# Rotary and norm products of an input projection: GpSimd or VectorE

## The chip, the cores and the metric

The kernel runs on one core of one Trainium2 chip (trn2). The metric is the device time of one execution in microseconds; lower is better. Before the change three runs took 3346.41, 3346.62 and 3347.53 us, a median of 3346.62 us.

A core has five engines that run side by side, each with its own queue of instructions, in order: TensorE (PE in the profile; its weight loads are PEld), VectorE (DVE), ScalarE (ACT), GpSimd (POOL) and SyncE (SP, which here only starts DMAs). GpSimd starts some DMAs too.

## The reference

Two layers of a hybrid diffusion backbone work on 128 context tokens and 1024 latent tokens with 1024 features. Cut to what matters:

```python
def _rms_norm(x, w):
    y = x * lax.rsqrt(jnp.mean(x * x, axis=-1, keepdims=True) + NORM_EPS)
    return y * w

def _rope_1d(x, pos):                      # rotate-half rotary over d dims
    ...
    return jnp.concatenate([x1 * cos - x2 * sin, x1 * sin + x2 * cos], axis=-1)

def _layer(x, cond, p, pos, ctx_kv):
    ...
    h = _rms_norm(x, p['norm1']) * (1 + sc1) + sh1
    proj = h @ p['w_in']                   # 1024 -> 2048
    q, k, v, zc, zh = jnp.split(proj, IN_SPLITS, axis=-1)
    q = _rms_norm(q.reshape(b, L, N_HEADS, HEAD_DIM), p['q_norm'])
    k = _rms_norm(k.reshape(b, L, N_KV_HEADS, HEAD_DIM), p['k_norm'])
    ...
    if pos is not None:                    # latent tokens
        q = _rope_2d(q, rows, cols)
        k = _rope_2d(k, rows, cols)
    attn_out = _blocked_attention(q, keys, vals)
    conv_out = _conformer_conv(zc, p)
    hy_out = _hyena(zh, p)
    mix = jnp.concatenate([attn_out, conv_out, hy_out], axis=-1) @ p['w_o']
    x = x + g1 * mix
    h2 = _rms_norm(x, p['norm2']) * (1 + sc2) + sh2
    ...                                    # ConvFFN, w_up and w_down
```

## The kernel before, in words

All activations lie transposed: 1024 features as 8 chunks of 128 partitions, 1152 tokens (128 context, then 1024 latent) along the free dimension, in three segments of 384 columns (`SEG`). Segment 0 holds both kinds of tokens, which have different modulation, so work that depends on it is cut there into 128 and 256 columns (`PARTS`). A matmul in full precision is made of three: each operand is split into a high part (`hh`, `whi`), rounded by a cast, and a low part (`hl`, `wlo`), the rest; `mm3` (L243) adds high x high, high x low and low x high.

Each layer has four phases. `phase1` (L1162) is the **input projection**: the norm of x, then 16 output tiles of 128 features, in the order that `ORDER` gives: six for the Hyena, then a q (0), k (4), v (5), and so on. `phase2` is the attention with the convolution beside it, `phase3` the output projection, `phase4` the ConvFFN. In the profiled execution phase 1 runs from about 85 to 408 us in layer 0 and from 1751 to 2068 us in layer 1.

**The norm.** `norm_seg` (L434) goes through the 8 chunks of a segment. R holds 1/rms of every token in all partitions. For most chunks VectorE forms x * A * R (`nt`, L450), ScalarE adds the shift B with a cast to the high part (`hh`, L451), and VectorE forms the low part (`hl`, L452). For chunks 2 and 5 (`norm_pool`, L149) the route is another: GpSimd multiplies x by R (L444), ScalarE applies A and B (L446) and casts the high part (L235), and GpSimd subtracts for the low part (L238). `norm_seg` is called from `phase1` with `which` = 0 and from `phase4` with `which` = 1, through `normed_dense2`, whose matmuls on the first two output tiles follow the chunks as they come.

**The rotations.** q (four tiles of two heads) and k (one) are scaled by `normed` (L1068): ScalarE squares and copies the matmul's result, TensorE sums the squares over 64 features and spreads the reciprocal roots, VectorE multiplies (L1090). Then `rope_out` (L1053) rotates the latent tokens of a segment: VectorE shuffles partitions into `sh` (L1060), GpSimd forms x * cos (L1061) and `sh` * sin (L1062), VectorE adds (L1063), `hilo` casts on ScalarE and subtracts on VectorE, and two DMAs on SP's queue store the parts (L1065, L1066). It is called 15 times per layer, 5 times on 256 columns and 10 times on 384.

**Order.** The framework orders each engine's instructions when the kernel is built, by priorities and a simulated timeline of its own; `high_priority` moves some ahead. Engines then work their queues in order. `tick` (L1181) interleaves the projection's matmuls with the rotation's steps and with those of the Hyena, whose own transforms (`hy_conv`, L826) also run on TensorE, with adds and products on VectorE.

**The seam.** After output tile 9 `open_attention` (L1244) takes memory that the Hyena frees and loads K with DMAs on GpSimd's queue (L1253 to L1258); `maxes` (L1329) loads q on SP's queue and starts the score matmuls (`S`, L1356).

Of the kernel before, what the change touches and what calls it, by code (L numbers as in the profile page):

```python
# [17 lines left out]
L = 1024  # L18
# [118 lines left out]
class Kern:  # L137
# [296 lines left out]
    def norm_seg(self, l, which, x, rr, hh, hl, s):  # L434

        nc, sh, g = self.nc, 0 if which == 0 else 24, self.nc.gpsimd
        a, b = SEG[s]
        R = self.rms_rows(rr)
        for c in range(8):
            y, xc = self.N("nt", "nw", 4), x(c, a, b)  # L440
            hi, lo = hh[c][:, a:b], hl[c][:, a:b]
            AB = [(u - a, v - a, self.aff[l][:, which, cond, c : c + 1], self.modT[l][:, cond, sh + c : sh + c + 1]) for cond, u, v in PARTS[s]]
            if c in self.norm_pool:
                self.mul(y[:], xc, R[:], g)  # L444
                for u, v, A, B in AB:
                    self.act(y[:, u:v], y[:, u:v], AF.Identity, scale=A, bias=B)  # L446
                self.hilo(hi, lo, y[:], lo_eng=g)
            else:
                for u, v, A, B in AB:
                    self.stt(y[:, u:v], xc[:, u:v], A, R[:, u:v], ALU.mult, ALU.mult)  # L450
                    self.act(hi[:, u:v], y[:, u:v], AF.Identity, bias=B)  # L451
                    self.stt(lo[:, u:v], y[:, u:v], B, hi[:, u:v].bitcast(F32), ALU.add, ALU.subtract)  # L452
# [599 lines left out]

    def rope_out(self, l, x, s, dst):  # L1053

        nc, g = self.nc, self.nc.gpsimd
        o, (a, b) = (128, (0, 256)) if s == 0 else (0, ((256, 640), (640, 1024))[s - 1])
        n = b - a
        x = x[:, o : o + n]
        sh, hi, lo = (self.N(t, "rp", 4, dt) for t, dt in (("sh", F32), ("rh", F32R), ("rl", F32R)))
        nc.vector.stream_shuffle(sh[:, :n], x, [(k + 16) % 32 for k in range(32)])  # L1060
        self.mul(x, x, self.cs[:, a:b], g)  # L1061
        self.mul(sh[:, :n], sh[:, :n], self.cs[:, L + a : L + b], g)  # L1062
        self.add(x, x, sh[:, :n])  # L1063
        self.hilo(hi[:, :n], lo[:, :n], x)
        nc.sync.dma_start(dst(0, a, b), hi[:, :n].bitcast(F32))  # L1065
        nc.sync.dma_start(dst(1, a, b), lo[:, :n].bitcast(F32))  # L1066
# [817 lines left out]
```

## Time and profile before

| | |
|---|---|
| median of three runs | 3346.62 us (3346.41 to 3347.53) |
| the profiled execution | 3345.59 us |
| its span, first to last instruction | 3343.3 us |
| TensorE busy | 3134.0 us, 94% of the span |
| VectorE busy | 2160.7 us, 65% |
| ScalarE busy | 1195.1 us, 36% |
| GpSimd busy | 495.1 us, 15% |
| mean granted TensorE clock | 0.958 of full speed |

How to read it: the busy time of an engine is the sum over its instructions, waits and DMA starts left out. "Releaser" or "<-" names what ended a wait by the semaphores. PEclk is the TensorE clock that was granted, as a share of full speed; its two levels are 1.2 and 2.4 GHz. A group's mean is over instructions of one form and one tile name.

### The profile page before, as it was taken

The numbers are of one execution on the slowest core, as the hardware profiler recorded it, in microseconds if no ns is written. First come the engines' busy times: TensorE is split into PE (matmuls) and PEld (weight loads), VectorE is DVE, ScalarE is ACT, GpSimd is POOL, SyncE is SP. The second block draws the span as 40 slices with busy tenths as digits, with TensorE's granted clock in tenths as the row PEclk, the third lists the DMA queues.
The fourth block names the chain that finished last, engine by engine and source line by source line (L and its number), as shares of the span: only waits on it lengthen the run. The fifth ranks groups of instructions, "written<-read, shape, count | busy, mean of one in ns | idle before, by whom it ended". The sixth has DMA issues, their size and how long they took to land. (4 is left out here: it accounts for less than half of the span.)

```text
span 3343.3 us, 44669 instructions
## 1 busy us (share of the span) xinstructions
PE 3134.0 (94%) x17330; PEld 2769.0 (83%) x17330; DVE 2160.7 (65%) x3464; ACT 1195.1 (36%) x1976; POOL 495.1 (15%) x412
## 2 busy tenths in 40 slices
PE   5899778999799999999998997899999999999997
PEld 3899733449799999999998995345799999999997
DVE  6887889665765554545567896987365454554556
ACT  3433333452352222333344333435343233333223
POOL 5402234221310000000012113422110000000002
PEclk8899879999899999999999997899999999999998
DMA  7565544445311111111113446351511111111112
GB/s 280 172 224 173 158 151 168 156 161 163 127 38 42 42 44 43 42 42 44 42 56 134 161 142 212 100 164 61 190 29 51 42 42 43 43 42 42 42 44 70
DMA packets 152327, 336.08 MB, mean 101 GB/s; under 512 B 21360, under 2 KB 57844, under 8 KB 145589
## 3 DMA queue, kind: packets, MB, share of 16 engines
q1 hardware_dynamic: 147412, 318.69, 29.8%
q0 software_dynamic: 4704, 14.55, 1.5%
q8 instruction: 137, 2.24, 0.3%
q14 instruction: 74, 0.60, 0.1%
HBM read 264.86 MB, written 68.31 MB: 100 GB/s over the span
## 5 line engine op out<-in xcount | busy, mean ns | idle before, releaser
L241 PE MATMUL up<-hl,whi 128*128 128x384 f32 (+1 forms) x2112 | 712.8, 338 | 4.4 <-DVE hl L227 2.9
L241 PE MATMUL up<-hh,whi 128*128 128x384 f32 (+1 forms) x2112 | 710.3, 338 | 3.6 <-ACT hh L212 2.7
L241 PE MATMUL up<-hh,wlo 128*128 128x384 f32 (+1 forms) x2112 | 711.9, 337 | 0.0
L215 DVE TENSOR_TENSOR wlo<-wraw,whi 128x512 fp32r<-128x512 f32 x362 | 255.6, 706 | 646.6 <-ACT whi L235 646.3
L235 ACT CAST whi<-wraw 128x512 fp32r<-128x512 f32 x362 | 223.7, 618 | 848.2 <-PE dn L241 358.1
L241 PEld LDWEIGHTS up<-hl,whi 128*128 128x128 f32 x2112 | 398.7, 189 | 6.4 <-DVE hl L227 4.3
L241 PEld LDWEIGHTS up<-hh,whi 128*128 128x128 f32 x2112 | 398.7, 189 | 4.3 <-ACT hh L212 3.1
L241 PEld LDWEIGHTS up<-hh,wlo 128*128 128x128 f32 x2112 | 398.8, 189 | 0.0
L227 DVE SCALAR_TENSOR_TENSOR xt<-dn,mod,xt 128x128 f32<-128x128 f32 (+2 forms) x704 | 332.5, 514 | 71.3 <-PE dn L241 71.1
L241 PE MATMUL dn<-gh,wlo 128*128 128x384 f32 (+1 forms) x1056 | 359.0, 340 | 0.0
L241 PE MATMUL dn<-gh,whi 128*128 128x384 f32 (+1 forms) x1056 | 358.1, 339 | 0.0
L241 PE MATMUL dn<-gl,whi 128*128 128x384 f32 (+1 forms) x1056 | 357.4, 338 | 0.0
L227 DVE SCALAR_TENSOR_TENSOR fu<-pd,vec,fu 128x1154 f32<-128x1154 f32 (+2 forms) x192 | 254.0, 1324 | 91.7 <-ACT fu L212 89.2
L215 POOL TENSOR_TENSOR acc<-acc,sq 128x384 f32<-128x384 f32 x51 | 55.0, 1087 | 1633.2 <-ACT sq L212 1632.2
L241 PE MATMUL win<-hl,whi 128*128 128x384 f32 x768 | 265.0, 345 | 9.5 <-DVE hl L227 5.5
L241 PE MATMUL win<-hh,whi 128*128 128x384 f32 x768 | 264.0, 347 | 3.4 <-ACT hh L235 1.1
L241 PE MATMUL win<-hh,wlo 128*128 128x384 f32 x768 | 263.8, 344 | 0.0
L1357 DVE TENSOR_REDUCE mx<-S 128x1 f32<-128x384 f32 x384 | 196.6, 548 | 37.4 <-PE S L241 36.5
L1678 ACT COPY pd<-up 128x384 f32<-128x384 f32 (+1 forms) x352 | 131.8, 401 | 239.1 <-PE up L241 239.1
L212 ACT ACTIVATE p<-st 128x1024 f32<-128x1024 f32 x144 | 147.1, 1022 | 158.3 <-PE st L241 157.9
L241 PEld LDWEIGHTS dn<-gl,whi 128*128 128x128 f32 x1056 | 199.9, 189 | 0.0
L241 PEld LDWEIGHTS dn<-gh,whi 128*128 128x128 f32 x1056 | 199.7, 189 | 0.0
(294 smaller groups left out, 5196.7 us busy)
## 6 DMA issues: line engine op xcount, KB each, us to landing
wmod<-in_w_mod SPq DMA_DIRECT2D x48, 1024.0 KB
wraw<-in_w_up SPq DMA_DIRECT2D x176, 256.0 KB
wraw<-in_w_dn SPq DMA_DIRECT2D x88, 256.0 KB
wraw<-in_w_in SPq DMA_DIRECT2D x64, 256.0 KB
q<-qD SPq DMA_DIRECT2D x48, 256.0 KB
mh<-mixD SPq DMA_DIRECT2D x16, 576.0 KB
ml<-mixD SPq DMA_DIRECT2D x16, 576.0 KB
khD<-fK SPq DMA_DIRECT2D x16, 512.0 KB
```

Of the source, the lines that this page charges most:

```text
L212: return self.nc.scalar.activation(out, in_, f, **k)
L215: return (eng or self.nc.vector).tensor_tensor(out, a, b, op=op)
L227: return (eng or self.nc.vector).scalar_tensor_tensor(out, a, s, b, op0=op0, op1=op1)
L235: self.nc.scalar.copy(hi, src)
L241: self.nc.tensor.matmul(out, l, r, start=start, stop=stop)
L1357: nc.vector.tensor_reduce(m3[:, k, s : s + 1], S[:, :384], op=ALU.max, axis=AX.X)
L1678: self.nc.scalar.copy(p[:, u + o : v + o], t[:, u - a : v - a])
```

## The change

In `norm_seg` the route over GpSimd is taken only for `which` = 1, so in the input projection all 8 chunks go over VectorE and ScalarE. In `rope_out` both products go to VectorE. Nothing else changes; in phase 4 and at the end GpSimd keeps its share.

```diff
@@ -440,7 +440,7 @@
             y, xc = self.N("nt", "nw", 4), x(c, a, b)
             hi, lo = hh[c][:, a:b], hl[c][:, a:b]
             AB = [(u - a, v - a, self.aff[l][:, which, cond, c : c + 1], self.modT[l][:, cond, sh + c : sh + c + 1]) for cond, u, v in PARTS[s]]
-            if c in self.norm_pool:
+            if which and c in self.norm_pool:
                 self.mul(y[:], xc, R[:], g)
                 for u, v, A, B in AB:
                     self.act(y[:, u:v], y[:, u:v], AF.Identity, scale=A, bias=B)
@@ -1052,14 +1052,14 @@
     def rope_out(self, l, x, s, dst):
 
-        nc, g = self.nc, self.nc.gpsimd
+        nc = self.nc
         o, (a, b) = (128, (0, 256)) if s == 0 else (0, ((256, 640), (640, 1024))[s - 1])
         n = b - a
         x = x[:, o : o + n]
         sh, hi, lo = (self.N(t, "rp", 4, dt) for t, dt in (("sh", F32), ("rh", F32R), ("rl", F32R)))
         nc.vector.stream_shuffle(sh[:, :n], x, [(k + 16) % 32 for k in range(32)])
-        self.mul(x, x, self.cs[:, a:b], g)
-        self.mul(sh[:, :n], sh[:, :n], self.cs[:, L + a : L + b], g)
+        self.mul(x, x, self.cs[:, a:b])
+        self.mul(sh[:, :n], sh[:, :n], self.cs[:, L + a : L + b])
         self.add(x, x, sh[:, :n])
```

## Rows read from the trace of the kernel before

**Rows 1.** Page, busy time of each engine over the span
```profile
PE 3134.0 (94%) x17330; PEld 2769.0 (83%) x17330; DVE 2160.7 (65%) x3464; ACT 1195.1 (36%) x1976; POOL 495.1 (15%) x412
```

**Rows 2.** Windows view: stretch, its length, busy time (instructions) of PE, PEld, DVE, ACT, POOL; PEclk, DMA, GB/s
```profile
91.00:127.00 36.00, 32.65 (x150) 29.43 (x151) 32.45 (x66) 22.98 (x49) 17.25 (x14) 0.85 0.63 192
236.00:408.00 172.00, 158.18 (x1049) 149.22 (x1045) 143.82 (x268) 60.56 (x112) 38.23 (x36) 0.92 0.51 162
261.00:268.00 7.00, 6.03 (x24) 4.97 (x25) 4.55 (x11) 1.79 (x4) 3.36 (x3) 0.50 0.29 95
1751.00:1790.00 39.00, 29.36 (x142) 26.06 (x141) 37.23 (x62) 25.05 (x55) 19.82 (x20) 0.89 0.59 216
1850.00:2020.00 170.00, 169.69 (x1117) 165.01 (x1115) 140.97 (x242) 59.83 (x105) 19.02 (x21) 1.00 0.46 146
2043.00:2050.00 7.00, 3.54 (x12) 2.66 (x9) 2.87 (x6) 0.00 (x0) 0.71 (x2) 0.50 1.02 236
```

**Rows 3.** Waits of PE, 236 to 408 us: total, times, longest
```profile
PE iy L241 <- ACT zh L235: 2.2, 1, 2.2
```

**Rows 4.** Waits of PE, 1700 to 2090 us
```profile
PE win L241 <- DVE hl L227: 4.8, 5, 1.4
...
PE S L241 <- issue: 3.4, 1, 3.4
...
PE win L241 <- POOL raw L730: 1.6, 1, 1.6
...
PE win L241 <- POOL hl L215: 1.2, 2, 0.7
PE win L241 <- ACT hh L235: 1.1, 1, 1.1
```

**Rows 5.** Groups by form, DVE, 1750 to 1790 us: busy, mean ns, idle before
```profile
L227 DVE SCALAR_TENSOR_TENSOR nt<-xt,aff,rms 128x384 f32<-128x384 f32 x12 | 9.6, 826 | 0.2 <-ACT rms L431 0.2
L227 DVE SCALAR_TENSOR_TENSOR hl<-nt,mod,hh 128x384 fp32r<-128x384 f32 x12 | 8.6, 735 | 1.4 <-ACT hh L212 1.3
L227 DVE SCALAR_TENSOR_TENSOR hl<-nt,mod,hh 128x256 fp32r<-128x256 f32 x6 | 4.4, 725 | 0.0
L227 DVE SCALAR_TENSOR_TENSOR nt<-xt,aff,rms 128x128 f32<-128x128 f32 x6 | 3.8, 636 | 0.0
```

**Rows 6.** Groups by form, DVE, 91 to 127 us
```profile
L227 DVE SCALAR_TENSOR_TENSOR nt<-x,aff,rms 128x256 f32<-128x256 f32 x6 | 2.8, 472 | 0.0
...
L227 DVE SCALAR_TENSOR_TENSOR nt<-x,aff,rms 128x128 f32<-128x128 f32 x6 | 1.9, 336 | 1.0 <-DMA x<-in_xT 1.0
```

**Rows 7.** Timeline of DVE, 1786 to 1788 us: start, duration
```profile
1786.14 0.61 DVE L227 SCALAR_TENSOR_TENSOR hl<-nt,mod,hh 128x384 fp32r<-128x384 f32 x1
1786.67 0.61 DVE L227 SCALAR_TENSOR_TENSOR nt<-xt,aff,rms 128x384 f32<-128x384 f32 x1
```

**Rows 8.** Groups by form, DVE, 200 to 408 us
```profile
L215 DVE TENSOR_TENSOR Y<-Y,W 128x512 f32<-128x512 f32 x16 | 12.0, 790 | 0.0
...
L215 DVE TENSOR_TENSOR nw<-nw,sh 128x384 f32<-128x384 f32 x10 | 5.6, 555 | 4.1 <-POOL sh L215 4.1
...
L215 DVE TENSOR_TENSOR f<-s 128x512 f32<-128x512 f32 x4 | 3.4, 885 | 0.0
...
L215 DVE TENSOR_TENSOR e<-isd 128x512 f32<-128x512 f32 x4 | 2.6, 686 | 0.0
...
L215 DVE TENSOR_TENSOR nw<-nw,sh 128x256 f32<-128x256 f32 x5 | 2.1, 417 | 1.5 <-POOL sh L215 1.5
```

**Rows 9.** Groups by form, POOL, whole span
```profile
L215 POOL TENSOR_TENSOR hl<-nt,hh 128x384 fp32r<-128x384 f32 x24 | 28.8, 1198 | 39.2 <-ACT hh L235 24.2 <-issue 11.4 <-PE rmsb L241 3.4
```

**Rows 10.** Timeline of DVE at the end of layer 1's projection
```profile
2033.38 0.28 DVE L215 TENSOR_TENSOR ml<-hyo,mh 128x128 fp32r<-128x128 f32 x1
```

**Rows 11.** Timeline of POOL at the end of layer 1's projection
```profile
2036.18 0.99 POOL L215 TENSOR_TENSOR sh<-sh,cs 128x384 f32<-128x384 f32 x1
2037.12 0.56 POOL L1253 DMA_DIRECT2D k<-kD  x1
```

## The prediction, made blind

> **What bounds the kernel now.** I read the page first: TensorE is busy for 94% of the span, GpSimd for 15% [rows 1]. So an edit that moves GpSimd's work to VectorE pays only where TensorE stands still or runs at its lower clock, and only the two input projections are touched. The windows view cuts these into stretches [rows 2]; read TensorE's busy time against the length, then the granted clock, then VectorE. Three kinds of place differ. In the norm of layer 1 (1751 to 1790) TensorE is idle for 9.6 of 39 us while VectorE is busy for 37.2: VectorE sets the pace. In the rotations and the Hyena work (236 to 408, 1850 to 2020) VectorE has 28 and 29 us free, and in layer 1 TensorE has no gap at all (169.7 of 170 us). At the seam to attention (2043 to 2050) TensorE has 3.5 us of work in 7 us, at a clock of 0.50, its 1.2 GHz level.
>
> The waits of TensorE say what ends those gaps. In layer 1's norm 4.8 us are ended by VectorE's low parts; 1.2 us by GpSimd's low parts, 1.1 by the ScalarE cast that follows GpSimd's product, and 1.6 are put down to a memset of GpSimd [rows 4]. No matmul reads that memset's tile; it sits in GpSimd's queue right behind a subtraction of the norm, so I count it as a third wait for GpSimd: 3.9 us in all. In layer 0 one Hyena matmul waits 2.2 us [rows 3], and the following 7 us run at 0.50 [rows 2]: 6.0 us of matmul time that would be about 3.0 at the upper level, so this one stall costs some 5.2 us.
>
> **The norm.** Per layer GpSimd loses 12 instructions (two chunks, three segments, a product and a subtraction) of 1.2 us [rows 9]. ScalarE's separate cast falls away, and VectorE gets 16: in segment 0 two operations on 128 and 256 columns for each chunk, in the others two on 384. By 0.336, 0.472 and 0.61 us [rows 6, 7] that is 4 x (0.336 + 0.472) + 8 x 0.61 = 8.1 us per layer. Neighbours start 0.53 us apart though each takes 0.61 [rows 7], so the queue grows by 16 x 0.08 us less: 6.8 us.
>
> Against it stands that VectorE is itself slowed while GpSimd works. Layer 1's groups have means far over the undisturbed durations [rows 5]: 12 x (0.826 - 0.61) + 12 x (0.735 - 0.61) + 6 x (0.725 - 0.472) + 6 x (0.636 - 0.336) = 2.6 + 1.5 + 1.5 + 1.8 = 7.4 us. Of the 20 GpSimd instructions in the stretch [rows 2], 12 are the norm's, 3 are memsets, and 5 add squares for the layer before and stay; so 12/17 of it comes back, 5.2 us. VectorE's queue grows by 6.8 - 5.2 = 1.6 us; the bounds are -0.6 (all 7.4 come back) and 6.8 (nothing does). The three waits for GpSimd go (3.9 us), and 1.6 us more of waiting for VectorE take their place: I take **2 us gained in layer 1**, bounds 6 gained and 3 lost. In layer 0 TensorE is idle for only 3.4 of 36 us, and filter matmuls fill its waits [rows 2]; VectorE's durations there are nearer the undisturbed ones [rows 6], so less comes back: **0.5 gained**, 2 either way.
>
> Trace view against skill: the rows show VectorE slowed by a part of GpSimd's time. The Trainium skill (Perfetto Trace Analysis, Optimizing Scalar/DVE Operations) says that moving work from a saturated VectorE even to GpSimd may make sense, though the two share a read port and it might not help. Its first half speaks against this change: with all 8.1 us per layer on the path the sum would be +16 us and not -2.5; its second half is what rows 5 show.
>
> **The rotations.** Five tensors in three segments per layer, two products each, leave GpSimd: 20 on 384 columns and 10 on 256. The sum that VectorE already does on the same tiles takes 0.555 and 0.417 us [rows 8]: 20 x 0.555 + 10 x 0.417 = 15.3 us per layer, 12.9 in the queue with the same overlap. Back come VectorE's waits for GpSimd's second product, 4.1 + 1.5 = 5.6 us in layer 0, and its slowed work: against 0.686 us, undisturbed, for 512 columns, 16 x (0.790 - 0.686) + 4 x (0.885 - 0.686) = 2.5 us in two groups alone [rows 8]. So the queue grows by at most 4.8 us in 172, where 28 are free [rows 2]: **nothing** on the path, covered by TensorE's own matmuls, and up to 4.8 us per layer if that cover goes. No semaphore wait is added: product and shuffle stand on one queue. Behind them wait the ScalarE cast, the low part and two stores on SP's queue; the stores are as many as before and become ready earlier. What can gain is the 5.2 us stall: slowed VectorE work precedes it, and a shorter chain frees the rotated tile's buffer sooner. I take **1.5 gained**, bounds 0 and 5.
>
> **The seam.** K's loads are issued on GpSimd's queue, behind rotations. In layer 1 the first goes out at 2037.12 us, as the last product in front of it ends [rows 11]; the Hyena buffer that it overwrites was read for the last time at 2033.4 [rows 10]. Without the products it can go 2 to 3 us sooner, and the score matmuls wait 3.4 us before they start [rows 4]. Late next are the q loads on SP's queue and the last q's chain. I take **2.5 gained**, bounds 0 and 3.4. In layer 0 I take nothing.
>
> **Sum.** -2 - 0.5 - 1.5 - 2.5 = -6.5 us. The profiled execution took 3345.59 us (span 3343.3), 1.03 under the median of 3346.62; a term shifts both alike, so it becomes 3339.1 and the median **3340**. A measurement of this kernel can tell about 0.2% from no change, 6.7 us: the forecast lies at that edge.
>
> **Rivals.** *No change* (3344 to 3350): VectorE, full in the norm already, takes over the waits that named GpSimd, and the K loads then wait for q's. For it: 4.8 us of waits name VectorE now [rows 4]. Against it: the seam's gain needs no free VectorE.
>
> *Slower*: the rotation's two products stand in VectorE's queue in front of the Hyena inverse transform on which TensorE's in-order matmuls wait, as in the one such stall of rows 3, and the lower clock follows. It decides if, ahead of such a matmul, the products add more than the GpSimd slowdown returns. At 5.2 us for a stall and one new one per layer: +10.4, less the seam's 2.5: 3354.5. For it: the instruction order is fixed when the kernel is built and changes with its instructions; layer 1 has no gap to lose into [rows 2]. Against it: 28 us free.
>
> *Much faster*: GpSimd blocks VectorE for its whole time, and the gaps I booked to VectorE are really GpSimd's. TensorE could then win up to its idle 9.6 and 3.4 us in the norms, the lower clock there (0.11 x 39 + 0.15 x 36 = 9.7 us), the stall's 5.2 and the seam's 3.4: 31 us, of which 25 would be much: 3322. Against it: 7.4 us of slowdown stand against 12 x 1.2 us of the norm's GpSimd time and the 5 others'. The Trainium skill (SBUF — State Buffer, SBUF: two separate sides) states such a lock between GpSimd and a VectorE operation with two SBUF inputs, held for a whole instruction; the trace agrees on the kind, since the sums on SBUF tiles are slowed, and shows about half the size.
>
> **Chances.** Forecast (3333 to 3344) 0.52, no change 0.18, slower 0.18, much faster 0.12. Of the forecast's 0.52 some 0.33 lie beyond 0.2%; with the much faster case that makes 0.45 faster. Its other 0.19 and 0.17 of the no-change case make 0.36 the same; 0.18 + 0.01 are slower. The range of 3327 to 3354 runs from the forecast's bounds added (-16, with some of the much faster case) to just under the slower case.
>
> **What would show it.** Right: in layer 1's norm the 384-column groups of VectorE fall from 826 and 735 ns to near 620, no wait of TensorE names GpSimd, and the stretch is 1 to 4 us shorter; VectorE's total rises by less than the added 46.7 us (2 x 8.1 + 2 x 15.3), by 10 to 25; K's first load goes out 2 to 3 us sooner after the Hyena's last read. Wrong: the waits for VectorE's low parts grow by over 4 us in a norm, TensorE's 169.7 of 170 us falls below 166, or new stretches at 0.50 appear in the rotations.

## The result, and the profile after

The kernel after takes 3326.57 us, the median of four runs (3323.58 to 3328.34), against 3347.07 us for four runs of before: a ratio of 0.9944, 95% interval 0.993 to 0.9959. A second comparison, six runs beside 22 of before, gave 3326.26 against 3343.86 us, 0.9938 (0.9926 to 0.995). By the medians the change gains 17.6 to 20.5 us. (A ratio here is taken over the runs of its comparison; it is not the quotient of the two medians, which would be 0.9939 and 0.9947.) The forecast was 6.5; the first median lies 0.4 us below the low end of the range, 3327, while its ratio applied to the forecast's starting value gives 3327.9.

The profiled execution took 3328.34 us, its span 3326.3, 17.0 less than before's. A second profile of the same kernel has a span of 3332.6. A single pair of profiles therefore prices nothing below some 6 us over the whole span; what several kernels show alike in one stage can be trusted further.

The page's busy times, after:

```profile
PE 3126.4 (94%) x17330; PEld 2763.4 (83%) x17330; DVE 2167.1 (65%) x3556; ACT 1188.7 (36%) x1964; POOL 400.8 (12%) x328
```

Beside [rows 1]: GpSimd loses 94.3 us. VectorE, to which the work went, gains only 6.4. By the durations of the forecast the moved work is 46.7 us, so by this estimate some 40 us came back from VectorE's other instructions. The page counts overlapping instructions once, though; with the forecast's own allowance for that the moved work is 39.4 us, and 33 came back.

The windows view, the stretches that answer to [rows 2] (layer 0's norm and rotations, two places in them where the clock fell for a part of the stretch, layer 1's norm and rotations):

```profile
91.00:127.00 36.00, 33.14 (x154) 29.65 (x154) 35.32 (x79) 20.23 (x44) 1.63 (x3) 0.86 0.68 214
236.00:404.00 168.00, 153.31 (x1021) 145.32 (x1019) 141.32 (x282) 60.69 (x108) 6.84 (x14) 0.93 0.54 168
258.00:266.00 8.00, 8.00 (x51) 6.72 (x50) 7.12 (x16) 3.16 (x6) 0.53 (x1) 0.79 0.68 199
290.00:298.00 8.00, 8.00 (x48) 8.00 (x47) 3.53 (x6) 3.89 (x7) 0.00 (x0) 0.79 0.49 166
1741.00:1776.00 35.00, 26.59 (x138) 23.89 (x137) 35.00 (x76) 21.59 (x48) 5.44 (x8) 0.90 0.66 244
1836.00:2006.00 170.00, 170.00 (x1116) 165.23 (x1115) 143.35 (x258) 57.00 (x104) 3.95 (x10) 1.00 0.47 151
```

VectorE is now full in layer 1's norm (35.00 of 35), and TensorE still has no gap in layer 1's rotations. Where before had one stall, at 261 us, this profile has two shorter dips of the clock, at 258 and 290. The lower clock in the norms has hardly lifted: 0.86 and 0.90, where it was 0.85 and 0.89.

Waits of TensorE, 1700 to 2090 us, after, beside [rows 4]:

```profile
PE ppt L251 <- DVE pp L1313: 5.0, 1, 5.0
PE mxt L251 <- DVE nmx L227: 4.1, 2, 2.6
PE nr L241 <- DVE nw L215: 3.7, 3, 2.1
PE win L241 <- DVE hl L227: 3.5, 4, 1.3
PE win L241 <- DVE wlo L215: 3.2, 1, 3.2
...
PE st L241 <- DMA q<-qD: 1.4, 1, 1.4
```

GpSimd is not named any more, and the wait for VectorE's low parts is 3.5 us (4.8 before). A wait of 3.2 us for the low part of a weight (`wlo`), also VectorE's, is new.

VectorE's groups by form in layer 1's norm, 1740 to 1776 us, after, beside [rows 5]:

```profile
L227 DVE SCALAR_TENSOR_TENSOR nt<-xt,aff,rms 128x384 f32<-128x384 f32 x16 | 9.0, 607 | 0.0
L227 DVE SCALAR_TENSOR_TENSOR hl<-nt,mod,hh 128x384 fp32r<-128x384 f32 x13 | 7.4, 608 | 0.0
L227 DVE SCALAR_TENSOR_TENSOR hl<-nt,mod,hh 128x256 fp32r<-128x256 f32 x8 | 4.5, 565 | 0.0
...
L227 DVE SCALAR_TENSOR_TENSOR nt<-xt,aff,rms 128x128 f32<-128x128 f32 x8 | 3.7, 466 | 0.0
```

The 826 and 735 ns of before are 607 and 608. The two smaller forms fell only to 565 and 466, not to the 472 and 336 that the forecast took from other tiles as undisturbed. The same in the rotations, 200 to 404 us, beside [rows 8]:

```profile
L215 DVE TENSOR_TENSOR Y<-Y,W 128x512 f32<-128x512 f32 x16 | 10.3, 680 | 0.0
...
L215 DVE TENSOR_TENSOR nw<-nw,cs 128x384 f32<-128x384 f32 x9 | 5.0, 552 | 0.1
L215 DVE TENSOR_TENSOR nw<-nw,sh 128x384 f32<-128x384 f32 x9 | 5.0, 551 | 0.1
```

**The seams.** GpSimd's timeline of before at the end of layer 0's projection, then that of after:

```profile
405.48 1.04 POOL L215 TENSOR_TENSOR sh<-sh,cs 128x384 f32<-128x384 f32 x1
406.47 0.57 POOL L1253 DMA_DIRECT2D k<-kD  x1
```

```profile
375.86 0.52 POOL L1253 DMA_DIRECT2D k<-kD  x1 [106.50 <-DVE hyo L215]
...
2002.18 0.56 POOL L1253 DMA_DIRECT2D k<-kD  x1 [156.70 <-PE iy L241]
```

K's first load goes out 30.6 us sooner in layer 0, 34.9 in layer 1 [rows 11], released by the Hyena's last use of that memory; TensorE's own work there is only 5 to 6 and 14 to 16 us ahead of before. The waits of TensorE from 385 to 420 us, before and after, show who is late next:

```profile
PE S L241 <- DMA k<-kD: 8.1, 1, 8.1
```

```profile
PE sp L241 <- DVE nw L215: 4.7, 1, 4.7
PE sp L241 <- ACT pp L212: 4.1, 1, 4.1
...
PE S L241 <- DMA q<-qD: 1.7, 1, 1.7
```

### The profile page after: what moved, and what is told of

Same layout as the page of the kernel before. It is cut to its first block, busy times and chain, and to the rows that moved or that the text cites. A ratio compares the mean times of both kernels' runs of the same rounds, so it can differ in the third digit from the quotient of the medians.

```text
span 3326.3 us, 44636 instructions
## 1 busy us (share of the span) xinstructions
PE 3126.4 (94%) x17330; PEld 2763.4 (83%) x17330; DVE 2167.1 (65%) x3556; ACT 1188.7 (36%) x1964; POOL 400.8 (12%) x328
## 3 DMA queue, kind: packets, MB, share of 16 engines
q1 hardware_dynamic: 147412, 318.69, 29.7%
## 5 line engine op out<-in xcount | busy, mean ns | idle before, releaser
L1678 ACT COPY pd<-up 128x384 f32<-128x384 f32 (+1 forms) x352 | 131.8, 401 | 239.6 <-PE up L241 239.6
```

What stands on the lines that cost most here:

```text
L1678: self.nc.scalar.copy(p[:, u + o : v + o], t[:, u - a : v - a])
```

## The experiments

Each ratio is to before, with its 95% interval. The kernels norm_shadow, k_late and the two q_early ran in another comparison, on another chip, than after_again; before's median was 3343.5 us in the one and 3343.9 in the other. A difference across the two rests on that agreement; by the ratios it comes out larger than by the medians. The table cuts one profile of each kernel at the first TensorE instruction into `win` (the projection), `iy` (the Hyena's inverse transform), `S` (the scores) and `up` (the ConvFFN) of each layer; `win` is the start itself, the other columns are the differences, in us, all worked out from those starts. The column S-up holds the attention, the output projection and the beginning of phase 4's norm.

| kernel | median of runs | to win | win-iy | iy-S | S-up | up-win | win-iy, layer 1 | iy-S | S-up | up-end |
|---|---|---|---|---|---|---|---|---|---|---|
| before | 3343.9 | 94.2 | 167.1 | 153.3 | 497.9 | 844.3 | 135.6 | 154.3 | 432.4 | 864.2 |
| after | 3326.6 | 92.4 | 162.9 | 154.4 | 493.1 | 844.2 | 131.8 | 152.2 | 430.9 | 864.4 |
| after_again | 3326.3 | 92.2 | 166.1 | 152.4 | 494.5 | 844.2 | 132.7 | 153.0 | 432.4 | 865.1 |
| norm_only | 3346.1 | 92.3 | 168.5 | 152.3 | 493.6 | 844.4 | 131.8 | 153.6 | 441.5 | 866.3 |
| rope_only | 3348.6 | 93.9 | 167.7 | 152.7 | 497.7 | 844.4 | 135.5 | 152.6 | 438.2 | 867.3 |
| rope_late | 3356.5 | 93.9 | 170.2 | 154.9 | 496.3 | 844.7 | 135.5 | 148.7 | 446.4 | 864.9 |
| k_on_act | 3351.4 | 93.1 | 166.8 | 153.6 | 494.4 | 844.2 | 135.4 | 154.2 | 439.4 | 864.1 |
| new_as_old | 3329.3 | 92.4 | 166.9 | 152.7 | 493.5 | 844.3 | 130.5 | 151.2 | 431.4 | 864.4 |
| old_as_new | 3349.1 | 94.3 | 169.7 | 154.8 | 494.8 | 844.3 | 135.8 | 152.9 | 437.5 | 864.3 |
| ropeg_as_new | 3339.3 | 92.2 | 163.6 | 155.1 | 497.3 | 842.6 | 131.8 | 152.4 | 437.3 | 864.4 |
| norm_shadow | 3337.0 | 92.5 | 169.1 | 152.6 | 494.9 | 844.5 | 135.9 | 152.7 | 430.2 | 864.4 |
| k_late | 3339.1 | 92.3 | 163.6 | 153.8 | 495.6 | 846.3 | 133.5 | 156.7 | 427.8 | 867.9 |
| q_early | 3327.2 | 89.7 | 163.0 | 152.1 | 495.2 | 844.2 | 131.7 | 154.7 | 428.7 | 864.2 |
| q_early_norms | 3324.4 | 93.0 | 166.1 | 151.9 | 492.7 | 840.3 | 131.7 | 156.7 | 428.9 | 862.3 |

(The profile of before is that of the first comparison, 3345.59 us; in the three comparisons here its median was 3343.5, 3343.7 and 3343.9.)

### Each half alone: norm_only, rope_only

```diff
-            if c in self.norm_pool:                               # norm_only
+            if which and c in self.norm_pool:
...
-        self.mul(x, x, self.cs[:, a:b], g)                        # rope_only, and L1062
+        self.mul(x, x, self.cs[:, a:b])
```

> Only the norm's half of the change; the rotations stay on GpSimd. Theory (each half acts by itself, in the places where the trace of after is ahead of the one of before: 3.4 us in layer 0's norm, 4.1 in layer 1's): 7 to 9 us below before, ratio 0.9973 to 0.998; K's first loads still go out at about 406 and 2037 us less the norm's own gain, so the seams stay as they were. Rival A (the norm is worth the 2.5 us that was forecast, the rest being a new order of instructions): ratio 0.999 or above. Rival B (GpSimd's slowdown of VectorE is all that counts, so the norm carries the larger part of the 20): ratio 0.9965 or below.

> Only the rotations' half; the norm keeps GpSimd for chunks 2 and 5. Theory: the seams gain 4 and 2 us, since K's loads go out some 25 to 35 us sooner, and part of the attention's 3.5 follows them: 6 to 12 us below before, ratio 0.9964 to 0.9982; with the norm alone it adds up to the whole change within 3 us. Rival A (the rotations give nothing, the seam having moved by the order of the build): ratio 0.9993 or above. Rival B (the halves need each other): the two gains add up to less than 15 of the 20 us.

Measured: norm_only 3346.11 us, ratio 1.0006 (0.9998 to 1.0015); rope_only 3348.58, 1.0016 (1.0007 to 1.0025). By the totals both theories fell. Rival A fits both ratios, and rival B of rope_only stood: the halves gain nothing alone. But the table shows the norm's gain in norm_only, 131.8 against 135.6 us in layer 1, and a loss elsewhere: layer 1's stage from S to up takes 441.5 and 438.2 us against 432.4, though norm_only moves no instruction there, and rope_only only the last q's four products behind the first score matmul. Two windows, from the first score matmul of layer 1 to the first output projection, before and norm_only:

```profile
2046.70:2373.20 326.50, 287.47 (x1240) 139.83 (x1241) 266.36 (x457) 142.25 (x201) 110.89 (x59) 0.92 0.44 140
```

```profile
2036.50:2370.50 334.00, 292.72 (x1240) 140.48 (x1241) 266.07 (x457) 142.67 (x201) 114.85 (x59) 0.89 0.41 136
```

The same 1240 matmuls on TensorE take 7.5 us longer, at a lower clock (0.89 against 0.92). What differs there by design is only the order in which the build interleaves them, and the moment at which they begin.

### K's place tried with the build's own order: rope_late, k_on_act

```diff
-        nc, g = self.nc, self.nc.gpsimd                                  # rope_late
+        nc, g = self.nc, None if self.late else self.nc.gpsimd           # late: the last two q
...
-            nc.gpsimd.dma_start(t[0:64, :].bitcast(F32), self.kD[0, r, :])   # k_on_act, and L1254, L1258
+            nc.scalar.dma_start(t[0:64, :].bitcast(F32), self.kD[0, r, :])
```

> Only the products of the last two q tiles (12 of 30 per layer), which stand in GpSimd's queue between the release of K's memory and K's loads, go to VectorE; those of k and of the first two q tiles, and the norm, stay on GpSimd. Theory (the gain of the rotations is K's place in GpSimd's queue): all of the gain of the whole rotation edit, within 2 us, with K's first load out near 376 us in layer 0. Rival (the gain is VectorE running undisturbed): 12 of 30 of it, about 2.5 to 5 us, in whatever place.

> The kernel before, with K's six loads per layer started by ScalarE in place of GpSimd; every rotation and norm stays on GpSimd. Theory (queue): K's loads go out long before 406 us and the seams gain 4 and 2 us, ratio 0.9976 to 0.9988, although GpSimd and VectorE do exactly the work they did. Rival (VectorE undisturbed): no gain, ratio 0.9993 or above. Third (ScalarE's own queue pays for a load that waits for memory): slower, with TensorE's waits naming ScalarE in the 30 us ahead of the seam.

Measured: rope_late 3356.52 us, 1.0037 (1.0025 to 1.005); k_on_act 3351.37, 1.0021 (1.0013 to 1.003). The theory of both fell, and so did rope_late's rival. In rope_late K's first load goes out at 392.80 us, not at 376. In layer 1 it goes out at 2007.27, 30 us sooner than before, and iy to S is the shortest of all kernels, 148.7 us; but the stage behind it takes 446.4, which is 14.0 more. In k_on_act ScalarE's queue gave K no earlier place, 405.07 us here and 2033.55 in layer 1, so it tells nothing of K. It was slower, as its third reading had it, but TensorE's wait for ScalarE ahead of layer 0's seam is the 2.3 us that it was before:

```profile
405.07 0.52 ACTq L1253 DMA_DIRECT2D k<-kD  x1
```

These four kernels differ from before by two things at once: where instructions run, and the order that the build makes of all the others. The next four part them.

### Engines and order apart: new_as_old, old_as_new, ropeg_as_new, after_again

The kernel is built twice. From a first build in one configuration the order of every engine is kept; in the second build each instruction that the change does not move is tied behind its predecessor in that order. The tie is one of issue order on one engine; it adds no wait. The moved instructions (`FREE`) find their own place.

```diff
+            traced = [i for i in nc.cur_bb.bb.instructions if i.name not in FREE]
+            for line in order or []:
+                for k, m in zip(line, line[1:]):
+                    tc.add_manual_dep(traced[m], traced[k].name, DEP, reason="order")
...
+    nc = built(*THIS, built(*LIKE)[1])[0]
```

> The whole change, but with every other instruction of every engine held in the order that the kernel before has; only the norm's and the rotations' moved instructions find their own places. Theory E (the engines: the gain is the norms' work going faster and K's loads going out sooner): ratio 0.995 to 0.997, with the layers' norm and seam stretches shorter as in after, and the attention no slower. Theory O (the order: what the build makes of the rest of the program, above all of the attention, decides): ratio 0.998 or above, the gain up to the second seam given back in the attention.

> The kernel before (norm chunks 2 and 5 and all rotation products on GpSimd), with every other instruction held in the order that after has. Theory E: no faster than before, ratio 0.999 to 1.002. Theory O: ratio 0.997 or below, as the order alone brings the larger part of 20 us. If both have a part, this ratio and that of the opposite kernel, new_as_old, multiply to about after's.

> The norm on VectorE, the rotations on GpSimd, in the order of after: against after it differs only in the rotations' engine. Theory E: 4 to 8 us slower than after, lost at the two seams (K's loads behind the products again). Rival (the rotations themselves are free, only the order they bring counts): within 2 us of after.

> The kernel after itself, on the same chip and against the same runs of before as its three variants. 0.9935 to 0.996 by the first comparison; an interval above 0.996 would mean that a chip shifts the ratio by as much as one of the parts.

| | order of before | order of after |
|---|---|---|
| norm and rotations on GpSimd | 3343.86 (before) | 3349.10, 1.0011 (1.0003 to 1.002) |
| norm on VectorE, rotations on GpSimd | | 3339.31, 0.9984 (0.9974 to 0.9994) |
| all on VectorE | 3329.34, 0.9957 (0.9945 to 0.9969) | 3326.26, 0.9938 (0.9926 to 0.995) |

Theory E holds in the main. With the order of before the engines alone gain 14.5 us. The new order alone gains nothing (it is 5.2 us slower), and with the new engines it adds 3.1, which is not shown, since the two intervals overlap. The ratios of new_as_old and old_as_new multiply to 0.9968 and not to after's 0.9938, so the two parts do not simply add up. In the table new_as_old differs from before by 1.8 (to win), 0.2, 0.6 and 4.4 in layer 0, and by 5.1, 3.1 and 1.0 in layer 1: about 7 for the norms, 9 for the seams and the attention behind them. Layer 1's stage from S to up, 431.4 us, is no longer worse, although it begins 15 us sooner; that points to their own order as what cost the halves their gain.

Read down the right column, the norm brings 9.8 us and the rotations 13.0. The second number is over the 4 to 8 us that were expected, and by the table it was not lost from iy to S (0.7 and 0.2 us against after) but from S to up (4.2 and 6.4). It is too large for what the change did, since after's order fits products on GpSimd badly. VectorE's timeline of old_as_new at layer 1's seam, then TensorE's:

```profile
2044.52 0.55 DVE L219 TENSOR_TENSOR nw<-nw,nr 128x384 f32<-128x384 f32 x1
2056.08 0.42 DVE L219 TENSOR_TENSOR rl<-nw,rh 128x256 fp32r<-128x256 f32 x1 [11.01 <-DMA qD<-rh]
2056.42 0.55 DVE L219 TENSOR_TENSOR nw<-nw,nr 128x384 f32<-128x384 f32 x1
2056.89 3.56 DVE L1366 TENSOR_REDUCE mx<-S 128x1 f32<-128x384 f32 x7
```

```profile
2057.49 0.69 PE L245 MATMUL S<-k,q 128*128 128x384 f32 x1 [9.17 <-DVE mx L1366]
```

A rotated tile's low part waits 11 us, by the profile until a store of a rotated tile is done; the maxima of the scores stand behind it on VectorE, and TensorE waits 9.2 us for them. ropeg_as_new has the same 9.2.

### Is it GpSimd at work, or a chain that is shorter: norm_shadow

In the kernel after, with its order held, GpSimd again does two passes for chunks 2 and 5, in segments 0 and 1, with results that nothing reads. The norm itself stays on VectorE.

```diff
+                if SHADOW and not which and s < 2 and c in self.norm_pool:
+                    z, h = hl[c][:, b : b + 384], hi.bitcast(F32)
+                    self.mul(z, h, h, g)
+                    self.sub(z, h, h, g)
...
```

> The kernel after, in its own order, with GpSimd made to run 8 products and subtractions of 128 x 384 per layer beside the input projection's norm again (chunks 2 and 5 of segments 0 and 1; operands are high parts that are ready, and the results go to places that the norm overwrites later, so nothing waits for them). The norm itself stays on VectorE. Theory (GpSimd at work slows VectorE, and that was most of what the norm gained, 9.8 us between the two kernels that differ in it alone): 3 to 7 us slower than after, ratio to before 0.9948 to 0.9963, with VectorE's 384-column groups of layer 1's norm back above 680 ns. Rival (the gain was the shorter chain of one chunk, three instructions of 1.2 us replaced by two of 0.6): within 2 us of after, ratio 0.9932 to 0.9946.

Measured: 3337.01 us, 0.9981 (0.9972 to 0.999), 10.7 us slower than after_again (14 by the two ratios): more than expected, and as much as all of the norm's gain (9.8). Layer 1's norm, 1740 to 1779 us, GpSimd's and VectorE's groups:

```profile
L219 POOL TENSOR_TENSOR hl<-hh 128x384 fp32r<-128x384 f32 x8 | 11.9, 1498 | 11.5 <-ACT hh L216 11.2
...
L231 DVE SCALAR_TENSOR_TENSOR hl<-nt,mod,hh 128x384 fp32r<-128x384 f32 x8 | 6.2, 822 | 0.0
L231 DVE SCALAR_TENSOR_TENSOR nt<-xt,aff,rms 128x384 f32<-128x384 f32 x9 | 5.6, 662 | 0.0
...
L231 DVE SCALAR_TENSOR_TENSOR nt<-xt,aff,rms 128x256 f32<-128x256 f32 x8 | 4.4, 553 | 0.0
L231 DVE SCALAR_TENSOR_TENSOR nt<-xt,aff,rms 128x128 f32<-128x128 f32 x8 | 4.3, 538 | 0.0
```

VectorE's low parts are back at 822 ns, where after_again has 606 in the same window. The two stages from win to iy taken together, first in after, then in norm_shadow (length, then busy times):

```profile
sum 294.70, PE 280.61 PEld 269.51 DVE 249.03 ACT 121.07 POOL 28.38; mean PE 140.30 PEld 134.75 DVE 124.51 ACT 60.53 POOL 14.19
```

```profile
sum 305.00, PE 287.62 PEld 275.22 DVE 257.21 ACT 121.13 POOL 58.03; mean PE 143.81 PEld 137.61 DVE 128.61 ACT 60.56 POOL 29.02
```

With the same 413 instructions VectorE is busy for 8.2 us more beside 29.7 us more of GpSimd. The stage win to iy of layer 1 is 135.9 us. That column divides all kernels: 135.4 to 135.9 in the six where GpSimd has the norm's passes or their shadow, 130.5 to 133.5 in the eight where it has not. The rival falls: no chain was lengthened here, and no wait of VectorE or TensorE in the two norms names GpSimd. Nor are the ties to blame: q_early, below, has the same ones and takes after's time.

### K's place alone: k_late

```diff
+        if s == 1 - l and last and LATE:
...
+            nc.gpsimd.tensor_copy(self.small([128, 1], "late")[:], x[:, 0:1])
+            late = nc.cur_bb.bb.instructions[-1]
...
+            for i in self.kload:
+                self.tc.add_manual_dep(i, late.name, DEP, reason="late")
```

> The kernel after, in its own order, with K's six loads per layer held on GpSimd's queue behind a copy of one column of the last q's rotated tile (its second segment in layer 0, its first in layer 1), about where the products kept them before. Theory (at the seams the rotations' gain is K's place in that queue): S waits for K again, the wait in layer 0 back from about 2 to 8 us, and 6 to 13 us slower than after, ratio to before 0.9955 to 0.9975. Rival (the seams gained because VectorE and the q's chain were faster, K being hidden anyway): within 2 us of after.

Measured: 3339.12 us, 0.9985 (0.9975 to 0.9994), 12.9 slower than after_again (16 by the two ratios). K's first loads go out at 395.60 and 2032.97 us, and the waits of TensorE at the two seams (385 to 425, then 2005 to 2070 us) are

```profile
PE S L245 <- DMA q<-qD: 7.4, 1, 7.4
...
PE S L245 <- DMA k<-kD: 7.6, 1, 7.6
```

The total is what the theory asked for, but the table does not give it to the seams. Against after's profile, iy to S and S to up together lose 1.9 us in layer 0 and 1.4 in layer 1 (4.5 lost, then 3.1 won back). Another 2.4 lie in the two norm columns, and 5.6 in the two ConvFFN stretches (846.3 and 867.9 us against 844.2 and 864.4), where the instructions are those of after; these I cannot explain. So K's place is shown to move the waits, and by the stages of this one profile it is worth some 3 us, not 13. In layer 0 that is too little: K went out 14.1 us ahead of the first S in k_late, but only 8.1 us ahead of it in before, so the copy did not bring back all of the delay. In layer 0 the late K loads did not make S wait for K but for q, whose loads now ran beside them.

### The next wait: q_early, q_early_norms

```diff
         nc, g, Q = self.nc, j // 2, []
+        n0, ld = len(nc.cur_bb.bb.instructions), nc.gpsimd if j == 0 and QG else nc.sync
...
-                nc.sync.dma_start(a[64 * k : 64 * k + 64, :].bitcast(F32), self.qD[j, 0, r, :])
-            nc.sync.dma_start(b[0:64, :].bitcast(F32), self.qD[j, 1, r, :])
+                ld.dma_start(a[64 * k : 64 * k + 64, :].bitcast(F32), self.qD[j, 0, r, :])
+            ld.dma_start(b[0:64, :].bitcast(F32), self.qD[j, 1, r, :])
...
-            if (which or NORM_G) and c in self.norm_pool:          # q_early_norms
+            if (which and not QG or NORM_G) and c in self.norm_pool:
```

> The kernel after, in its own order, with the six loads of the first q (per layer) on GpSimd's queue right behind K's, in place of SP's, where they stand behind the mix stores until 405 us. Theory (now that K comes early, q's loads are what the first score matmuls wait for last): the waits of S and st for q go, 1.4 to 4.3 us a layer, and the time falls 2 to 6 us below after, ratio to before 0.992 to 0.9935. Rival (the last q's own chain of norm and rotation ends at the same time, so another wait takes its place): within 1.5 us of after.

> As q_early, and phase 4's norm loses its GpSimd route as well (chunks 2 and 5 on VectorE and ScalarE in all norms but the last one). Theory (the same slowdown acts there): 1 to 4 us below q_early, as TensorE's two waits for GpSimd's low parts (0.6 and 1.1 us) go. Rival (phase 4's first matmuls wait for VectorE anyway): within 1 us of q_early or slower, the wait for VectorE's low parts (2.8 us) growing.

Measured: q_early 3327.20 us, 0.995 (0.9938 to 0.9963); the rival stood. Its waits from 385 to 425 us:

```profile
PE sp L245 <- DVE nw L219: 6.5, 1, 6.5
PE sp L245 <- ACT pp L216: 3.9, 1, 3.9
```

S no longer waits for q (`st` still does, 1.3 us); the prompt attention's matmul `sp`, ahead of it in TensorE's queue, waits for VectorE's `nw` instead, 6.5 us where it was 4.7. q_early_norms took 3324.37 us, 0.9941 (0.9928 to 0.9953), 2.8 below q_early, within the theory's 1 to 4, though the two intervals overlap. Phase 4 is 3.9 and 1.9 us shorter than q_early's in the columns up to win and up to end, and its wait for VectorE's low parts did not grow (2.1 us in layer 0, 2.8 in after). In these two profiles, q_early and q_early_norms, the other columns lose as much again, and the spans are alike (3323.5 and 3323.6). Its interval and that of after overlap as well; 1.9 us between their medians are no proof of a better kernel. It is the lowest median of all.

## Why the prediction was right and wrong

**Direction and place: right.** The gain lies where TensorE stood still. No wait names GpSimd; 607 and 608 ns stand where near 620 was forecast; layer 1's rotations still fill 170.0 of 170 us, so their products on VectorE cost nothing there.

**The norm: the mechanism was right, the size was not.** "I take 2 us gained in layer 1" was 2.9 and 3.8 in after's two profiles and 5.1 in new_as_old, and layer 0, taken at 0.5, gave 2 with the order held, most of it ahead of the first matmul (92.4 against 94.2 us), and 6 and 3 by after's two profiles. The step that failed is "VectorE's queue grows by 1.6 us". From win to iy of layer 1 VectorE is busy for 108.5 us in before and for 108.1, 108.3 and 107.7 in after, after_again and new_as_old: with 15 or 16 more instructions its queue did not grow. The three waits of 3.9 us, less nothing in place of less 1.6, come near what was measured. (In after's order the new wait for `wlo`, 3.2 us, stands against them; new_as_old has none.) I had priced the slowdown from four groups only, 7.4 us, of which 1.3 were no slowdown (565 and 466 ns stand after, not 472 and 336), and had given back 12/17 of it. norm_shadow shows that GpSimd at work beside the norm costs as much as the whole gain. The page shows VectorE's total up by 6.4 us, where I had 10 to 25. My bound of 6 held layer 1.

**The stall: not shown.** "I take 1.5 gained" rested on a chain that frees a buffer sooner. The wait of 2.2 us is 1.4 in after and 2.0 in new_as_old. From 255 to 300 us the clock is 0.92 in both and 0.96 in after_again, against 0.89; but the stretch at 0.50 near 293 us is a new one, which the forecast called a sign of being wrong. From iy to S the three take 154.4, 152.7 and 152.4 us against 153.3. A gain of 1.5 us is neither shown nor excluded.

**Layer 1's seam: about right, for a half-right reason.** 2.5 was forecast; iy to S is shorter by 2.1 and 1.3 in after's two profiles and 3.1 in new_as_old. It is 1.9 shorter in ropeg_as_new too, where the products are on GpSimd and K goes out at 2025.96 us, so this column alone does not show whose gain it is; k_late, with 4.5 more than after, speaks for K. K's load did not go out 2 to 3 us sooner; beyond the 14 us of all work there it went out 21 us sooner. I had taken the reading of `ml` at 2033.4 us [rows 10] for the last use of K's memory; in after the same last `ml` runs at 2023.87 us, 22 us behind K's first load at 2002.18, so it is not what K waits for. Late next were q's loads, as the forecast said.

**Layer 0's seam: the step that failed most.** "In layer 0 I take nothing" left out a wait of 8.1 us for K that stood in the trace of before. I had not read the waits around 414 us, and the same misreading of the release hid that K could come early. With the order held, iy to S and S to up gain 5.0 us there. K's place alone is worth about 2 of them by k_late's stages; how the rest divides between VectorE undisturbed and fewer transfers at once is open.

**What had no term.** The build orders the whole program anew for each change. In after that is worth 3.1 us at most by the medians, and not shown to be anything. In norm_only, rope_only, rope_late and k_on_act layer 1's stage from S to up is 6 to 14 us longer; norm_only had been 10.2 us ahead at the first S of layer 1 and lost 9.1 behind it, the other three had been 2 to 5 ahead and lost more than that. Why those orders are slower I did not follow.

**The sum.** With the order held the profiles give 7 us for the norms, 9 for the seams and the attention behind them, against 2.5 and 2.5 in the forecast, with 1.5 for the stall. The terms' bounds added up to 16 us, and the result went past them: the norm and the seam of layer 1 came near theirs, and layer 0's seam, taken as nothing, had been given no bound at all.

**The rivals.** *No change* is out by its interval. *Slower* asked for products ahead of a transform's matmul and a new stall per layer; there are 170.0 of 170 us in layer 1. Its argument that the order changes with the instructions did come true, in the partial kernels. *Much faster*, 3322, was 4.6 us off the result, the forecast 13.4, and it had a part of the mechanism: GpSimd's work was behind more of the norms' gaps than I had booked to it. But the lower clock in the norms, 9.7 us of its sum, stayed for the most part, and its condition, VectorE blocked for GpSimd's whole time, is not met: an estimated 33 to 40 us came back for 94.3 us of GpSimd's time, 35 to 43%, and norm_shadow has 8.2 us for 29.7. The Trainium skill (SBUF — State Buffer, SBUF: two separate sides) tells of a lock held for a whole instruction; the trace agrees on who slows whom, and shows under half of GpSimd's time as loss. It does not decide whether single instructions lock each other, since not every GpSimd instruction has a VectorE one beside it.

## What to carry to other kernels

Ask of a busy GpSimd not how much it does but what VectorE does meanwhile: if VectorE sets the pace there, moving the work onto VectorE itself can shorten the stage. Before an edit is judged by its total, hold the order of all other instructions; otherwise the build's new order can hide a gain of the same size. And read the waits at every seam of both layers, with the event that truly releases the memory.

## What the hardware showed unexpectedly

- GpSimd instructions whose results nobody waits for cost the program 10.7 us in norm_shadow: eight of 2460 ns in layer 0's norm and eight of 1498 ns in layer 1's, while VectorE's 384-column low parts there went from 608 to 822 ns.
- A queue's transfers need not be the ones that are named late: with K's loads issued beside q's in k_late, S waited 7.4 us for q (1.7 in after).
- In k_late's ConvFFN TensorE lost 5.6 us without a wait or a lower clock in the windows of its profile (1.00). In one stretch, about 1215 us, its matmuls start 0.177 us apart, where after's start 0.173 apart. I have no cause for it.
